# LN1's second transposes ahead of the last first-half products, weight sums behind its normalisation, residual offset added in the second f1/f2 chunk

## The chip, the cores and the metric

The kernel runs on one core of a Trainium2 chip. A core has a matrix engine (TensorE, PE), a vector engine (VectorE, DVE), a scalar engine (ScalarE, ACT), a general engine (GpSimd, POOL), and SyncE (SP), which here only issues loads. Each engine works through its own queue of instructions in order and waits on semaphores for the others. DMAs are issued from the queues of SP, ACT and POOL. The metric is the device time of one execution, in microseconds (us), as the median of several runs.

## What is computed

One layer of a decoder on 512 tokens of width 1024: a layer norm, a token mixer (gated linear attention beside latent attention), and a dense network, both with a scaled residual. The end of the reference, where the change lies:

```python
h = layer_norm(x, ln_in_g, ln_in_b)
mix = token_mixer(h, cos, sin, w_in[l], ...)
h = layer_norm(DEEPNORM_ALPHA * h + mix, ln1_g[l], ln1_b[l])
ff = jnp.square(jax.nn.relu(h @ w_ff1[l])) @ w_ff2[l]
h = layer_norm(DEEPNORM_ALPHA * h + ff, ln2_g[l], ln2_b[l])
```

`w_ff1` is 1024 x 4096 and `w_ff2` 4096 x 1024; `DEEPNORM_ALPHA` is 2 to the power 1/4.

## The kernel before

**Arithmetic.** Products are made of float32 operands split in two parts: `hi` is the operand rounded to the matrix engine's float32r, `lo` the rest. A product is hi·hi + hi·lo + lo·hi, so three matmuls (L245 to L247). Weights come by SP in tiles of 128 x 1024 (512 KB), and `pump` splits each one: ACT writes `whi` (L189), DVE subtracts to make `wlo` (L190).

**Order.** The program is written as a main thread that issues the matmuls, with generators beside it (`spawn`, `tick`, `finish`) that issue evictions, norms and transposes a step at a time. A scheduler then fixes the order of each engine's queue. `tc.issue_after(x)` makes what is written under it come behind the instruction x in that order. Once the queues are built, each is worked off in order.

**LN1.** After the mixer's output projection, `res` holds four tiles of 128 tokens by 1024. `ln1(0)` norms and transposes the tiles 0 and 1 (tokens 0 to 255, the first half), `ln1(1)` the tiles 2 and 3. In each, `ln_rows` takes mean and variance on DVE, raises the variance to the power −1/2 on POOL (L428) and normalises in place on DVE (L434). `ln_transpose` then makes, for each of eight k, two 128 x 128 transposes on PE (L443), the scaled `hi` on ACT (L446), an unrounded copy on ACT or DVE (L448, L450) and `lo` on DVE (L451). The results `h1T[k]` are the operand of f1.

**f1 of chunk 0.** While `ln1(1)` runs, PE does the f1 products of the first half: `gemm_fm` with `toks=slice(0, 256)`, eight k by four output blocks by three matmuls, 96 in all, each 256 wide. The same blocks are then run for the second half.

**f1 and f2 in chunks.** The hidden width of 4096 is taken in four chunks of 1024 (`FC = 4`). A chunk has f1 in blocks (`F1`), then f2. In the chunks 0 to 2, f2 is done by a scheme of seven products over quarters of the weight (`WIN`: 11, 21, T1, T2, T4, 22, T3). Its sums of quarters, T1 to T3, are made by `win_sums` on DVE (L1407), three for each half hf, and T4 during the products (L1460). The quarters are loaded by POOL's queue (`win_load`, L1399): chunk 0's before, those of chunk ci + 1 during f2 of chunk ci. From chunk 1 on the sums are held back behind the last evacuation of f2 (`st["ev"]`); those of chunk 0 aren't. The sums of hidden values are made by `win_hid` on DVE, and split by ACT and DVE (`xh`, `xl`).

**Evacuation.** Each of the seven products ends in two PSUM tiles. ACT copies each to an `ev` tile (L1471), and POOL issues one or more accumulating DMAs (L1473) that add it onto a 128 x 512 half of a `res` tile in SBUF. A chunk has 16 such DMAs of 256 KB.

**Residual.** `residual1` turns `res` from normalised rows to the scaled residual: it broadcasts `ln1_g` and `ln1_b` over the partitions by two DMAs on ACT's queue (`bcast_row`, L106), scales both by ALPHA on DVE (L1363, L1364), and multiplies each `res` tile by `bg` (L1365, L1369) and adds `bb` (L1370), all before f2 of chunk 0 starts. Addition onto `res` is commutative up to rounding, so the offset may be added at any time before the last norm.

Of the kernel before, what the change touches and what calls it, by code (L numbers as in the profile page):

```python
# [15 lines left out]
AF = mybir.ActivationFunctionType  # L16
ALU = mybir.AluOpType
AX = mybir.AxisListType

P = 128  # L20
T = 512
D = 1024
NT = T // P
# [12 lines left out]
ALPHA = 2.0 ** 0.25  # L36
# [16 lines left out]
def tile_hybrid_block(ctx: ExitStack, tc: tile.TileContext, I, out, dbg=None):  # L53
    nc = tc.nc
# [18 lines left out]
    def A(shape, dt=F32, n="a"):  # L73
        tag, bufs = ("C", 8) if n in TAG_C else (n, TAG_W[n]) if n in TAG_W else ("A", 24)
        return pa.tile(shape, dt, tag=tag, bufs=bufs, name=nm(n))

    def B(shape, dt=F32, n="b"):
        return pb.tile(shape, dt, tag="B", name=nm(n))

    def S(shape, dt=F32, n="s"):  # L80
        return sm.tile(shape, dt, tag=n, name=nm(n))
# [5 lines left out]
    def MM(n="mm"):  # L87
        return pm.tile([P, T], F32, tag="mm", name=nm(n))

    def PX(shape=(P, T), dt=F32, n="px"):  # L90
        return px.tile(list(shape), dt, tag="px", name=nm(n))

    def f(ap):
        return ap.bitcast(F32)

    act = nc.scalar.activation
    vtt = nc.vector.tensor_tensor
    vts = nc.vector.tensor_scalar
    stt = nc.vector.scalar_tensor_tensor
    gtt = nc.gpsimd.tensor_tensor  # L100
    mm = nc.tensor.matmul

    def bcast_row(name):
        t = A([P, D], F32, "bc")
        src = I[name]
        nc.scalar.dma_start(t, bass.AP(tensor=src.tensor, offset=src.offset, ap=[[0, P], [1, D]]))  # L106
        return t
# [21 lines left out]
    ident = ca[:, 0:P]  # L129
# [10 lines left out]
    st = {"dma": 0, "spl": 0, "gates": ()}  # L140
# [59 lines left out]
    def weights(pl, k):  # L200
        per = pl["per"]
        i = pl["idx"][k // per]
        pump(i)
        hi, lo = stream[i]["w"]
        return hi[:, k % per, :], lo[:, k % per, :]
# [4 lines left out]
    def spawn(g):  # L210
        active.append(g)
        return g
# [9 lines left out]
    def tick(width):  # L222
        for g in list(active[:width or WID[0]]):
            step(g)

    def finish(*gs):
        while any(g in active for g in gs):
            for g in list(active):
                if g in gs:
                    step(g)  # L230

    def part(x, i, c):
        return x[i][:, c] if isinstance(x, tuple) else x[:, i, c]

    def gemm_fm(pl, xs, n, evac, width=None, toks=slice(0, T), accs=None, guard=None):
        na = n // P
        accs = accs or [MM() for _ in range(na)]
        for k in range(pl["nk"]):
            hi, lo = weights(pl, k)
            xh, xl = part(xs[k], 0, toks), part(xs[k], 1, toks)  # L240
            first, last = k == 0, k == pl["nk"] - 1
            for a in range(na):
                c = slice(a * P, (a + 1) * P)
                o = accs[a][:, toks]
                mm(o, hi[:, c], xh, start=first, stop=False)  # L245
                mm(o, hi[:, c], xl, start=False, stop=False)  # L246
                mm(o, lo[:, c], xh, start=False, stop=last)  # L247
            if not last:
                tick(width)
        if guard:  # L250
            guard()
        if evac is not None:
            for a in range(na):
                evac(a, accs[a])
                if a == na // 2 - 1:
                    pump(pl["idx"][-1] + 1)
        tick(width)
        return accs
# [41 lines left out]
    PL = {}  # L300
# [121 lines left out]
    def ln_rows(src, dst, mv, on_act=False):  # L422
        bst = S([P, 2, 6], F32, "bst")
        for j in range(2):
            nc.vector.bn_stats(bst[:, j, :], src[:, j * T:(j + 1) * T])
        nc.vector.bn_aggr(mv, bst)
        vts(mv[:, 1:2], mv[:, 1:2], LN_EPS, None, op0=ALU.add)  # L427
        gtt(mv[:, 1:2], mv[:, 1:2], mhalf[:, 0:1], op=ALU.pow)  # L428
        if on_act:
            nmr = S([P, 1], F32, "nmr")  # L430
            stt(nmr, mv[:, 0:1], -1.0, mv[:, 1:2], op0=ALU.mult, op1=ALU.mult)
            act(dst, src, AF.Identity, scale=mv[:, 1:2], bias=nmr)
        else:
            vts(dst, src, mv[:, 0:1], mv[:, 1:2], op0=ALU.subtract, op1=ALU.mult)  # L434

    def ln_transpose(rows, g, b, outs, hf, alt=False, n="h0"):
        tk = slice(hf * 256, (hf + 1) * 256)
        for k in range(NK):
            if len(outs) <= k:
                outs.append(A([P, 2, T], F32R, n) if n == "h0" else (B([P, T], F32R, n), B([P, T], F32R, n)))  # L440
            p = MM() if alt and k in (4, 5) else PX()
            for i in range(2):
                nc.tensor.transpose(p[:, i * P:(i + 1) * P], rows[2 * hf + i][:, k * P:(k + 1) * P], ident)  # L443
            tmp = B([P, 256], F32, "lnt")
            hi, lo = part(outs[k], 0, tk), part(outs[k], 1, tk)
            ha = act(hi, p[:, :256], AF.Identity, scale=g[:, k:k + 1], bias=b[:, k:k + 1])  # L446
            if (alt or n == "h1") and k % 2:
                act(tmp, p[:, :256], AF.Identity, scale=g[:, k:k + 1], bias=b[:, k:k + 1])  # L448
            else:
                vts(tmp, p[:, :256], g[:, k:k + 1], b[:, k:k + 1], op0=ALU.mult, op1=ALU.add)  # L450
            hd = vtt(lo, tmp, f(hi), op=ALU.subtract)  # L451
            if n == "h1":
                st["ln"] = (ha, hd)
            yield hd
# [4 lines left out]
    def ln_in0():  # L459
        for tt in range(2):  # L460
            ln_rows(xt[tt], xt[tt], mvin[:, tt, :], on_act=tt == 0)
        yield from ln_transpose(xt, g_in, b_in, hT, 0, alt=True)
# [458 lines left out]
    scale = HQ ** -0.5  # L921
# [371 lines left out]
    t0, mv = mla_pair(0)  # L1293
# [3 lines left out]
    t1, mv = mla_pair(1)  # L1297
    mv(lambda: finish(*t0))
    t2, mv = mla_pair(2)
    mv(lambda: finish(*t1))  # L1300
    t3, mv = mla_pair(3)
    mv(lambda: finish(*t2))
    y_mla(0)
    res = []
# [33 lines left out]
    h1T = []  # L1338

    def ln1(hf):  # L1340
        for tt in (2 * hf, 2 * hf + 1):
            mv = S([P, 2], F32, "mv")
            ln_rows(res[tt], res[tt], mv)
        yield
        for k, _ in enumerate(ln_transpose(res, ln1g, ln1b, h1T, hf, n="h1")):
            if k % 2:
                yield
# [5 lines left out]
    finish(t_ln)  # L1353
    st["gates"] = st["ln"]
    t_ln = spawn(ln1(1))
    accs = gemm_fm(PL["f1", 0, 0], h1T, T, None, toks=slice(0, 256))
    finish(t_ln)

    def residual1():
        bg, bb = bcast_row("ln1_g"), bcast_row("ln1_b")  # L1360
        yield
        with tc.issue_after(st["ln"][1].ins):
            vts(bg, bg, ALPHA, None, op0=ALU.mult)  # L1363
            vts(bb, bb, ALPHA, None, op0=ALU.mult)  # L1364
            vtt(res[0], res[0], bg, op=ALU.mult)  # L1365
        yield
        for tt in range(NT):
            if tt:
                vtt(res[tt], res[tt], bg, op=ALU.mult)  # L1369
            vtt(res[tt], res[tt], bb, op=ALU.add)  # L1370
            yield

# [29 lines left out]
    def win_sums(ci):  # L1402
        def held(*a, **kw):
            with ExitStack() as gates:
                if "ev" in st:
                    gates.enter_context(tc.issue_after(st["ev"].ins))
                vtt(*a, **kw)  # L1407
        for hf in range(2):
            q12 = WQ.pop((("f2", ci), ("12", hf)))
            t1 = WQ[("f2", ci), ("T1", hf)] = A([P, 2, T], F32, "T1")  # L1410
            held(t1, q12, WQ[("f2", ci), ("11", hf)], op=ALU.subtract)
            yield
            held(q12, WQ[("f2", ci), ("22", hf)], q12, op=ALU.subtract)
            WQ[("f2", ci), ("T3", hf)] = q12
            yield
            t2 = WQ[("f2", ci), ("T2", hf)] = A([P, 2, T], F32, "T2")
            held(t2, q12, WQ[("f2", ci), ("11", hf)], op=ALU.add)
            yield
# [88 lines left out]
    for ci in range(FC):  # L1507
# [19 lines left out]
        for b, w in F1[ci]:  # L1527
            if ci == 0 and b == 0:
                gemm_fm(PL["f1", ci, b], h1T, T, ev_h, toks=slice(256, T), accs=accs)
                t_r1 = spawn(residual1())  # L1530
            else:
                gemm_fm(PL["f1", ci, b], h1T, w * P, ev_h, width=2)
            if win and b == 0:
                t_ws = spawn(win_sums(ci))
        if ci == 0:
# [6 lines left out]
        else:  # L1542
# [16 lines left out]
            rows = []  # L1559
# [7 lines left out]
            bg, bb = rows  # L1567
# [6 lines left out]
            tt, r, bst = 3, res[3], S([P, 4, 6], F32, "bst4")  # L1574
# [3 lines left out]
            for c0, n in ((0, T), (T, 256), (T + 256, 256)):  # L1578
                last = c0 > T
                acc = end if last else MM()[:, :n]  # L1580
                ws = slice(c0 % T, c0 % T + n)
                for k in range(nb):
                    hi, lo = weights(PL["f2last"][c0 // T], k)
                    xh, xl = hid[k][:, 0, tt * P:], hid[k][:, 1, tt * P:]
# [58 lines left out]
```

## Time and profile before

| what | value |
|---|---|
| median of three runs | 890.56 us (889.98 to 890.59) |
| time of the profiled execution | 890.77 us |
| its span in the profile | 888.9 us |
| granted TensorE clock | 0.999 |
| instructions | 12959 |

The profiled execution's time is 1.9 us longer than its span, which runs from the first to the last recorded instruction. All stamps below are microseconds from the span's start. A row of a timeline gives start, length, engine, line, operation, output <- inputs, shapes and count, and in brackets the idle time of the engine before it and what ended it. A row of the DMA view gives destination <- source, the issuing queue, the number of DMAs, the size of each and the median time from issue to landing. An engine's busy time is measured on its own; whether it costs anything is seen only where PE, the engine that is nearly always busy, waits.

### The profile page before, as it was taken

What the parts mean: (1) busy time and instruction counts of PE and PEld (TensorE: products, weight loads), DVE (VectorE), ACT (ScalarE), POOL (GpSimd) and SP (SyncE); (2) the same over time, 40 slices, a digit from 0 to 9 for tenths busy, and PEclk for the clock granted to TensorE, in tenths of its full rate; (3) what the DMA queues carried; (4) which work ended last, traced back from release to release, by engine and by line L of the source; (5) the groups of instructions that cost most, each with busy time, mean ns of one, the idle gap of its engine ahead of it and who ended that gap; (6) DMA issues with size and microseconds to landing.
All of it is one profiled execution on the core that took longest, in us unless ns stands there. A gap on an engine that the chain in (4) does not pass through costs nothing.

```text
span 888.9 us, 12959 instructions
## 1 busy us (share of the span) xinstructions
PE 870.0 (98%) x4844; PEld 757.6 (85%) x4844; DVE 629.8 (71%) x1011; ACT 468.8 (53%) x824; POOL 181.0 (20%) x198
## 2 busy tenths in 40 slices
PE   5999999999999999999999999999999999999996
PEld 5988887888899988888888888988888888889985
DVE  7859878967366745647766697887557646788865
ACT  5556666655366543535654424465457546656810
POOL 0324456725021010100000003004400520131001
PEclk9999999999999999999999999999999999999999
DMA  7995938234879433121307618005940990399312
GB/s 236 282 230 148 326 86 247 72 86 106 283 166 247 128 101 101 42 55 53 111 9 284 190 51 305 1 1 147 301 121 19 264 257 30 81 228 237 118 62 82
DMA packets 88414, 130.92 MB, mean 147 GB/s; under 512 B 8944, under 2 KB 50800, under 8 KB 88352
## 3 DMA queue, kind: packets, MB, share of 16 engines
q1 hardware_dynamic: 69120, 91.83, 32.7%
q0 software_dynamic: 17312, 34.61, 18.0%
q10 hardware_dynamic: 1920, 3.66, 1.1%
q8 instruction: 38, 0.62, 0.3%
q14 instruction: 24, 0.20, 0.1%
HBM read 108.58 MB, written 8.91 MB: 132 GB/s over the span
## 4 chain that ended last, share of the span: by engine, by line
PE 93%; POOL 2%; DVE 2%; issue 1%; DMA 1%; ACT 1%; POOLq 0%; SPq 0%; DVEq 0%; ACTq 0%
PE mm L245 12%; PE mm L247 12%; PE mm L246 12%; PE mm L279 6%; PE mm L281 6%; PE mm L280 6%; PE mm L1174 3%; PE mm L1173 3%; PE mm L1172 3%; PE px L1454 2%; PE px L1455 2%; PE px L1456 2%; PE mm L1455 2%; PE mm L1454 2%; PE mm L1456 2%; POOL rp L786 1%
## 5 line engine op out<-in xcount | busy, mean ns | idle before, releaser
L190 DVE TENSOR_TENSOR wlo<-wraw,whi 128x1024 fp32r<-128x1024 f32 (+2 forms) x93 | 103.9, 1118 | 98.8 <-ACT whi L189 93.8
L189 ACT ACTIVATE whi<-wraw 128x1024 fp32r<-128x1024 f32 (+2 forms) x93 | 88.7, 953 | 91.9 <-PE mm L246 40.4
L245 PE MATMUL mm<-h,whi 128*128 128x512 f32 x256 | 100.0, 391 | 0.0
L246 PE MATMUL mm<-h,whi 128*128 128x512 f32 x256 | 99.8, 390 | 0.0
L247 PE MATMUL mm<-h,wlo 128*128 128x512 f32 x256 | 95.2, 390 | 0.0
L190 DVE TENSOR_TENSOR wlo<-wq,whi 128x1024 fp32r<-128x1024 f32 x44 | 54.2, 1232 | 27.5 <-ACT whi L189 27.5
L1473 POOL DMA_DIRECT2D res<-ev x42 | 37.0, 1003 | 179.8 <-ACT ev L1471 146.2
L189 ACT ACTIVATE whi<-wq 128x1024 fp32r<-128x1024 f32 x44 | 46.4, 1056 | 23.7 <-PE mm L1173 9.9
L247 PEld LDWEIGHTS mm<-h,wlo 128*128 128x128 f32 x256 | 48.0, 188 | 10.3 <-DVE wlo L190 0.4
L245 PEld LDWEIGHTS mm<-h,whi 128*128 128x128 f32 x256 | 48.1, 188 | 9.8
L246 PEld LDWEIGHTS mm<-h,whi 128*128 128x128 f32 x256 | 48.1, 188 | 9.7
L1172 PE MATMUL mm<-sh,whi 128*128 128x256 f32 x160 | 45.4, 284 | 0.0
L1174 PE MATMUL mm<-sh,wlo 128*128 128x256 f32 x160 | 45.4, 284 | 0.0
L1173 PE MATMUL mm<-sh,whi 128*128 128x256 f32 x160 | 45.3, 283 | 0.0
L189 ACT ACTIVATE xh<-wraw 128x1024 fp32r<-128x1024 f32 (+1 forms) x28 | 27.2, 982 | 28.4 <-PE mm L281 15.7
L428 POOL TENSOR_TENSOR mv<-mv,mhalf 128x1 f32<-128x1 f32 x4 | 3.3, 838 | 170.5 <-DVE mv L427 170.5
L792 ACT ACTIVATE E<-rp 128x256 f32<-128x256 f32 x64 | 26.1, 419 | 22.3 <-POOL rp L787 13.8
L190 DVE TENSOR_TENSOR xl<-wraw,xh 128x1024 fp32r<-128x1024 f32 (+1 forms) x28 | 31.3, 1129 | 9.0 <-ACT xh L189 8.9
L1516 ACT ACTIVATE relu<-mm 128x512 f32<-128x512 f32 x24 | 14.1, 595 | 41.9 <-PE mm L247 41.9
L787 POOL TENSOR_TENSOR rp<-rp 128x256 f32<-128x256 f32 x32 | 32.3, 1010 | 11.6 <-ACT q L817 8.9
L786 POOL TENSOR_TENSOR rp<-rp 128x256 f32<-128x256 f32 x32 | 29.3, 916 | 20.2 <-ACT E L792 10.8
L794 DVE TENSOR_TENSOR M<-E,qk 128x512 f32<-128x512 f32 x32 | 28.9, 907 | 5.9 <-ACT E L792 5.9
(453 smaller groups left out, 2731.7 us busy)
## 6 DMA issues: line engine op xcount, KB each, us to landing
wraw<-in_w_ff_dram SPq DMA_DIRECT2D x36, 512.0 KB, 5.1
wraw<-in_w_in_dram SPq DMA_DIRECT2D x33, 512.0 KB, 4.0
wq<-in_w_ff_dram POOLq DMA_DIRECT2D x26, 512.0 KB, 9.7
res<-ev POOLq DMA_DIRECT2D x42, 256.0 KB, 10.0
wq<-in_w_in_dram SPq DMA_DIRECT2D x16, 512.0 KB, 6.2
wq<-in_w_in_dram POOLq DMA_DIRECT2D x16, 512.0 KB, 8.9
hsd<-hs SPq DMA_DIRECT2D x16, 256.0 KB, 4.1
xr<-hsd SPq DMA_DIRECT2D x16, 256.0 KB, 4.9
```

What stands on the lines that cost most here:

```text
L189: st["ins"] = act(hi[:, :nk, :n], raw[:, :nk, :n], AF.Copy)
L190: st["lo"] = vtt(lo[:, :nk, :n], raw[:, :nk, :n], f(hi[:, :nk, :n]), op=ALU.subtract)
L245: mm(o, hi[:, c], xh, start=first, stop=False)
L246: mm(o, hi[:, c], xl, start=False, stop=False)
L247: mm(o, lo[:, c], xh, start=False, stop=last)
L279: mm(o, xh, hi[:, :n], start=opens, stop=False, skip_group_check=share)
L280: mm(o, xh, lo[:, :n], start=False, stop=False, skip_group_check=share)
L281: mm(o, xl, hi[:, :n], start=False, stop=last, skip_group_check=share)
L786: gtt(Rv[:, :, 0, :], Rv[:, :, 0, :], Pv[:, :, 1, s - 1:s].to_broadcast([P, n, s]), op=ALU.add)
L1172: mm(oa, hi[:, k, c], xh, start=opens and k == 0 and a == 0, stop=False, skip_group_check=True)
L1173: mm(oa, hi[:, k, c], xl, start=False, stop=False, skip_group_check=True)
L1174: mm(oa, lo[:, k, c], xh, start=False, stop=k == 3, skip_group_check=True)
```

## The change

The change has three parts. (1) `gemm_fm` can hold its products from some k on behind an instruction; in the first-half f1 call the products of k = 6 and 7 (24 of 96) come behind the second half's transposes of k = 3. (2) The sums of chunk 0's weight quarters come behind LN1's last normalise. (3) `residual1` only multiplies by the gain; the offset's broadcast, its scaling (on ACT now, not DVE) and the four adds are made by a generator of their own, `offset1`, which is started in chunk 1 after the first f1 block's matmuls are issued.

```diff
+    def gemm_fm(pl, xs, n, evac, width=None, toks=slice(0, T), accs=None, guard=None, behind=None):
...
-            for a in range(na):
-                c = slice(a * P, (a + 1) * P)
-                o = accs[a][:, toks]
-                mm(o, hi[:, c], xh, start=first, stop=False)
...
+            with ExitStack() as gates:
+                if behind and k >= behind[0]:
+                    gates.enter_context(tc.issue_after(st[behind[1]].ins))
+                for a in range(na):
+                    c = slice(a * P, (a + 1) * P)
+                    o = accs[a][:, toks]
+                    mm(o, hi[:, c], xh, start=first, stop=False)
...
-            vts(dst, src, mv[:, 0:1], mv[:, 1:2], op0=ALU.subtract, op1=ALU.mult)
+            return vts(dst, src, mv[:, 0:1], mv[:, 1:2], op0=ALU.subtract, op1=ALU.mult)
...
-                nc.tensor.transpose(p[:, i * P:(i + 1) * P], rows[2 * hf + i][:, k * P:(k + 1) * P], ident)
+                t = nc.tensor.transpose(p[:, i * P:(i + 1) * P], rows[2 * hf + i][:, k * P:(k + 1) * P], ident)
+            if k == 3:
+                st["tr"] = t
...
-            ln_rows(res[tt], res[tt], mv)
+            st["aff"] = ln_rows(res[tt], res[tt], mv)
...
-    accs = gemm_fm(PL["f1", 0, 0], h1T, T, None, toks=slice(0, 256))
+    accs = gemm_fm(PL["f1", 0, 0], h1T, T, None, toks=slice(0, 256), behind=(6, "tr"))
...
     def residual1():
-        bg, bb = bcast_row("ln1_g"), bcast_row("ln1_b")
+        bg = bcast_row("ln1_g")
         yield
         with tc.issue_after(st["ln"][1].ins):
             vts(bg, bg, ALPHA, None, op0=ALU.mult)
-            vts(bb, bb, ALPHA, None, op0=ALU.mult)
             vtt(res[0], res[0], bg, op=ALU.mult)
         yield
+        for tt in range(1, NT):
+            vtt(res[tt], res[tt], bg, op=ALU.mult)
+            yield
+
+    def offset1():
+        bb = bcast_row("ln1_b")
+        yield
+        act(bb, bb, AF.Copy, scale=ALPHA)
+        yield
         for tt in range(NT):
-            if tt:
-                vtt(res[tt], res[tt], bg, op=ALU.mult)
             vtt(res[tt], res[tt], bb, op=ALU.add)
             yield
...
-                if "ev" in st:
-                    gates.enter_context(tc.issue_after(st["ev"].ins))
+                gates.enter_context(tc.issue_after(st["ev" if "ev" in st else "aff"].ins))
                 vtt(*a, **kw)
...
+            if ci == 1 and b == 0:
+                spawn(offset1())
             if win and b == 0:
                 t_ws = spawn(win_sums(ci))
```

More of the change, by code (lines that the diff above doesn't have):

```diff
@@ L233, in part @@
         return x[i][:, c] if isinstance(x, tuple) else x[:, i, c]
-    def gemm_fm(pl, xs, n, evac, width=None, toks=slice(0, T), accs=None, guard=None):
+    def gemm_fm(pl, xs, n, evac, width=None, toks=slice(0, T), accs=None, guard=None, behind=None):
         na = n // P
@@ L241, in gemm_fm @@
             first, last = k == 0, k == pl["nk"] - 1
-            for a in range(na):
-                c = slice(a * P, (a + 1) * P)
-                o = accs[a][:, toks]
-                mm(o, hi[:, c], xh, start=first, stop=False)
-                mm(o, hi[:, c], xl, start=False, stop=False)
-                mm(o, lo[:, c], xh, start=False, stop=last)
+            with ExitStack() as gates:
[5 more added lines that the diff above has]
+                    mm(o, hi[:, c], xh, start=first, stop=False)
+                    mm(o, hi[:, c], xl, start=False, stop=False)
+                    mm(o, lo[:, c], xh, start=False, stop=last)
             if not last:
```

## The prediction

> **What bounds the kernel now.** I read the page first: totals, the chain that ended last, the DMA issues.
>
> ```profile
> span 888.9 us, 12959 instructions
> PE 870.0 (98%) x4844; PEld 757.6 (85%) x4844; DVE 629.8 (71%) x1011; ACT 468.8 (53%) x824; POOL 181.0 (20%) x198
> PE 93%; POOL 2%; DVE 2%; issue 1%; DMA 1%; ACT 1%; POOLq 0%; SPq 0%; DVEq 0%; ACTq 0%
> res<-ev POOLq DMA_DIRECT2D x42, 256.0 KB, 10.0
> ```
>
> TensorE (PE) is busy for 98% of the span and carries 93% of the chain. The change removes no product, so it can gain only where PE stands still and lose only where it makes PE stand still. Next the table by stretches of time (columns: stretch, length, then PE, PE weight load, DVE, ACT, POOL busy us with counts, granted clock, DMA share, GB/s), for LN1 with the first f1 products, for the end of chunk 0's f1, and for chunk 1's f1.
>
> ```profile
> 548.50:566.00 17.50, 17.15 (x140) 16.58 (x139) 14.52 (x27) 6.30 (x12) 1.85 (x2) 1.00 0.29 103
> 575.00:596.00 21.00, 21.00 (x95) 17.37 (x93) 19.95 (x30) 13.57 (x23) 0.00 (x0) 1.00 0.00 1
> 640.00:680.00 40.00, 40.00 (x178) 33.16 (x177) 21.65 (x30) 23.16 (x35) 3.60 (x5) 1.00 0.40 98
> ```
>
> PE idles only in the first stretch: 17.50 − 17.15 = 0.35 us, more than that when counted start to start, because the end of a matmul is modelled. In the third, PE takes one 512-wide product every 40.00/178 = 0.225 us and never stops. The timeline of PE in LN1 shows the stall (start, length, instruction, and in brackets the idle time before it and its releaser).
>
> ```profile
> 560.13 0.29 PE L247 MATMUL mm<-h,xl 128*128 128x256 f32 x1
> 560.26 1.03 PE L443 MATMUL px<-ca,res 128*128 128x128 f32 x8
> 561.62 0.74 PE L245 MATMUL mm<-h,xh 128*128 128x256 f32 x4 [0.33 <-ACT h L446]
> 562.20 0.44 PE L443 MATMUL px<-ca,res 128*128 128x128 f32 x2
> 562.66 0.39 PE L246 MATMUL mm<-h,xh 128*128 128x256 f32 x1
> 562.88 0.28 PE L247 MATMUL mm<-h,xl 128*128 128x256 f32 x1
> 563.72 0.64 PE L245 MATMUL mm<-h,xh 128*128 128x256 f32 x4
> ```
>
> The 96 first-half products end at 560.13 with a product's pitch of 560.26 − 560.13 = 0.13 (0.12 where they run in rows). Eight transposes of the second half follow, and the products of that half wait for ACT's eviction of them. Eight transposes at some 0.108 last until 561.13, so 0.49 is lost before 561.62; the smaller steps up to 563.72 (four products at 0.12 from 561.62 to 562.10 with the transposes only at 562.20, and three like it) add some 0.45. The stall is about 0.95 us.
>
> **The change, part by part.** *(1) Gate on the last 24 first-half products, weight sums behind the normalisation.* The second half's transposes of k = 0 to 3 go ahead of the 24 products of k = 6 and 7, so these 24 × 0.12 = 2.9 us cover the evictions that were waited for. That needs the normalised rows by 560.26 − 2.9 = 557.4. DVE and POOL in that place:
>
> ```profile
> 553.99 1.85 POOL L428 TENSOR_TENSOR mv<-mv,mhalf 128x1 f32<-128x1 f32 x2 [9.93 <-DVE mv L427]
> 554.20 1.22 DVE L1407 TENSOR_TENSOR T<-wq,wq 128x1024 f32<-128x1024 f32 x1
> 555.46 1.23 DVE L1407 TENSOR_TENSOR wq<-wq,wq 128x1024 f32<-128x1024 f32 x1
> 556.60 1.53 DVE L434 TENSOR_SCALAR res<-res,mv 128x1024 f32<-128x1024 f32 x2
> ```
>
> POOL's two pow end at 555.84. The two normalises are over at 558.13, because a weight sum (to 556.69) runs ahead of them. Behind the gate on them the sums come after, and 555.84 + 1.53 = 557.4, with the first row tile done half of that earlier: just in time. Transposes issue at the same count, earlier; no DMA moves. I take the whole 0.95 (bounds 0 and 0.95). The sums are pushed back 1.5 us on a DVE that has their products due only in f2, after 596.
>
> *(2) Offset out of residual1.* DVE loses there one bias scale and four adds:
>
> ```profile
> 568.13 0.69 DVE L1364 TENSOR_SCALAR bc<-bc 128x1024 f32<-128x1024 f32 x1
> 573.27 3.49 DVE L1370 TENSOR_TENSOR res<-res,bc 128x1024 f32<-128x1024 f32 x3
> 577.81 1.22 DVE L1370 TENSOR_TENSOR res<-res,bc 128x1024 f32<-128x1024 f32 x1
> ```
>
> That is 0.69 + 3.49 + 1.22 = 5.4 us of DVE between 568 and 579, while PE does not stop (21.00 busy of 21.00 behind it): worth nothing by itself.
>
> *(3) The adds in chunk 1.* Between 568 and 579 nothing wrote `res`. In chunk 1 the accumulating DMAs of f2's chunk 0 write it, and each add of a res tile waits until the last of these has landed. POOL's issues of that chunk, the tile view's row of the last six (shortest, median and longest issue in ns, first and last start), and the times to landing of the first and of the last of these:
>
> ```profile
> 607.98 1.84 POOL L1473 DMA_DIRECT2D res<-ev  x2 [52.15 <-ACT ev L1471]
> 615.22 5.30 POOL L1399 DMA_DIRECT2D wq<-in_w_ff_dram  x7
> 637.49 0.85 POOL L1473 DMA_DIRECT2D res<-ev  x1 [5.65 <-DMA res<-ev]
> 639.26 4.35 POOL L1473 DMA_DIRECT2D res<-ev  x5 [0.92 <-DMA res<-ev]
> L1473 POOL DMA_DIRECT2D res<-ev x6: 847/1151/1862, 637.5 to 642.5; - x6
> res<-ev POOLq DMA_DIRECT2D x1, 256.0 KB, 6.5
> res<-ev POOLq DMA_DIRECT2D x1, 256.0 KB, 10.3
> ```
>
> The last six land from 637.49 + 6.5 = 644.0 to 642.5 + 10.3 = 652.8, so 8.8/5 = 1.76 apart: a stream at its own pace. In DVE's new order these adds stand in line with chunk 1's f1 weights: the fourth add (res[3]), then one weight sum, then the subtraction that makes `wlo` of an f1 weight tile; I call it tile E. DVE is in order, so all of it waits for the last landing. Its slack:
>
> ```profile
> 640.81 1.23 DVE L190 TENSOR_TENSOR wlo<-wraw,whi 128x1024 fp32r<-128x1024 f32 x1 [3.44 <-ACT whi L189]
> 646.28 1.23 DVE L190 TENSOR_TENSOR wlo<-wraw,whi 128x1024 fp32r<-128x1024 f32 x1 [4.24 <-ACT whi L189]
> 650.62 0.39 PE L245 MATMUL mm<-h,whi 128*128 128x512 f32 x1
> 651.53 0.62 PE L247 MATMUL mm<-h,wlo 128*128 128x512 f32 x2
> ```
>
> Tile E's first product is the row at 650.62. Its `wlo` was ready at 647.51 and PE first needs it at 651.53: 4.0 us of slack. With a landing at L it is ready at L + 1.22 (add) + 1.22 (sum) + 1.23 less two overlaps of 0.08 = L + 3.5. If L stayed at 652.8, that is 656.3 and PE stands until then: +4.8 against today, whatever LN1 gained, because the end of this wait is set by DMA, not by PE. The tile before it (subtracted at 640.81, due 24 products of 0.225 before tile E's, at 646.1) has the first add ahead of it: 644.0 + 1.22 + 1.23 = 646.4 at worst, 0.3 late and swallowed by the next wait.
>
> *(4) What moves L.* The new order of PE brings the first evacuation of f2 chunk 0 behind 36 products, not 48: 12 × 0.225 = 2.7 us earlier, plus 0.95 from LN1. ACT and POOL there:
>
> ```profile
> 604.31 2.00 ACT L189 ACTIVATE xh<-T 128x1024 fp32r<-128x1024 f32 x2
> 607.08 1.09 ACT L1471 ACTIVATE ev<-px 128x512 f32<-128x512 f32 x2 [0.78 <-PE px L1456]
> 612.47 0.60 ACT L1471 ACTIVATE ev<-px 128x512 f32<-128x512 f32 x1 [1.17 <-DMA res<-ev]
> ```
>
> The second pair of evacuations waits for the first pair's landing, and the seven weight loads and the rest of POOL's queue come after it. So a first pair 3.4 us earlier (3.65 less a split that is now ahead of it on ACT for part of it) brings L to 652.8 − 3.4 = 649.4, unless ACT is held in between. And ACT now has, before that second pair, the scale of `bb`, which waits for its own 512 KB broadcast, issued by ACT at about 602.4 (one `xh` split of 1 us ahead of the row at 604.31, less 0.95). Bounds of its price: the four bc loads of before, and an SP load of equal size on quiet queues.
>
> ```profile
> bc<-in_ln_in_g_dram ACTq DMA_DIRECT2D x1, 512.0 KB, 8.0
> bc<-in_ln_b_dram ACTq DMA_DIRECT2D x2, 512.0 KB, 10.0
> wraw<-in_w_ff_dram SPq DMA_DIRECT2D x1, 512.0 KB, 3.8
> L1314 ACT ACTIVATE bc<-bc x1: 1060/1060/1060, 480.1 to 480.1; 128x1024 f32<-128x1024 f32 x1
> ```
>
> The first two ran beside other loads. At 602 the queues are quiet (0.00 DMA share up to 596) but for one SP load that comes at about the same time, so I take a value near the quiet end, 3.8 to 5.2. At 3.8 it lands at 606.2, when ACT is done with the evacuations (605.6): ACT loses 1.06 + 0.6, which its idle time before 607.08 and 612.47 (0.78 + 1.17) covers. L = 649.4, `wlo` ready at 652.9, net 652.9 − 651.5 = +1.4. At 5.2, 607.6: the second pair comes some 1.2 later, L = 650.6, net +2.6. I forecast between: +1.8, that is 890.77 + 1.8 = 892.6 for the profiled run, which lies 0.2 above the median, and so 892.4.
>
> [...]
>
> **Rivals.** *A: ACT is held by the broadcast.* It takes the loaded price, 8.0 to 10.0: it lands at 610.4 to 612.4, `bb` is scaled by 611.5 to 613.5, two more splits (1.05 each) follow, and the second pair evacuates at 613.6 to 615.6 instead of 612.47, so L is 1.1 to 3.1 later than before: net +5.9 to +7.9; between this and the forecast (a landing at 608 to 610) lies +3 to +5. For it: all bc rows. Against it: quiet queues. About 894 to 898.5.
>
> *B, the other side: the slack takes the adds.* From L below 651.53 − 0.95 − 3.5 = 647.1 on PE does not wait and only the gain of LN1 is left: 890.56 − 0.95 = 889.6. The stream would have to run 5.7 us earlier, by the two pairs' waits falling away altogether; for it stands that landings, not work, delay the second pair (1.17 idle); against it the 1.76 spacing behind POOL's seven loads.
>
> *C: the gate does not do what it says.* The normalises are ready later than 557.4 (the pow rows, 1.85 for two, are rough), PE waits on the transposes instead of the evictions. LN1 gains nothing; L is 0.95 later; net +2.4 to +3.5: 893.0 to 894.1.
>
> **How the numbers follow.** Forecast 0.55 (891.8 to 893.2), A with what lies between 0.27, B 0.12, C 0.06. The range runs from B's 889.6 to 896.5, into A: about 0.12 is left out above and 0.04 below. A difference under 0.2% (1.8 us, below 888.8 or above 892.3) is what a measurement here can't tell from none. Faster by more would need twice LN1's stall: 0.04. B and the lower half of the forecast are "same": 0.40. The upper half, A and C: 0.56.
>
> **What would show it.** In the new profile: no idle time of PE over 0.2 us between 555 and 566 (part 1); the normalises ahead of the sums; the add of res[3] on DVE released by a DMA res<-ev at 649 to 651, and a PE idle time of 2 to 4 us before the wlo product near 651 to 654, released by DVE wlo; ACT's scale of `bc` idle before it under 2 us (A: over 4). The prediction is wrong if PE has no idle time there (B), if L is later than 651.5 (A), or if a stall appears in another place, such as the T sums due in f2.

## The result, and the profile after

| | before | after |
|---|---|---|
| median, us | 890.61 (889.98 to 891.03, 6 runs) | 894.93 (894.37 to 895.39, 6 runs) |
| profiled execution, us | 890.77 | 895.39 |
| its span, us | 888.9 | 893.4 |

The changed kernel is slower: ratio 1.0048, 95% interval 1.0038 to 1.0058, or 4.3 us. The forecast was 892.4 within 889.6 to 896.5.

The page of the changed kernel, the totals, the chain that ended last, and the group of products with `wlo` (busy us, mean ns | idle time before them, releaser):

```profile
span 893.4 us, 12964 instructions
PE 872.0 (98%) x4844; PEld 758.6 (85%) x4844; DVE 629.1 (70%) x1010; ACT 470.5 (53%) x825; POOL 181.6 (20%) x198
PE 82%; issue 7%; DMA 5%; POOL 3%; DVE 2%; ACT 1%; POOLq 0%; SPq 0%; DVEq 0%; ACTq 0%
L250 PE MATMUL mm<-h,wlo 128*128 128x512 f32 x256 | 96.1, 394 | 3.7 <-DVE wlo L190 3.7
```

PE still does 4844 instructions, but its share of the chain fell from 93% to 82%, and DMA, 1% before, now has 5%: the chain now runs back through transfers for part of the way. The products with `wlo` idle 3.7 us for DVE, where they idled for nothing before.

**LN1.** The timeline of PE and then of DVE in the changed kernel:

```profile
556.98 1.04 PE L446 MATMUL px<-ca,res 128*128 128x128 f32 x8
560.72 0.38 PE L446 MATMUL px<-ca,res 128*128 128x128 f32 x2
560.85 0.60 PE L248 MATMUL mm<-h,xh 128*128 128x256 f32 x3
561.29 0.82 PE L446 MATMUL px<-ca,res 128*128 128x128 f32 x6
561.86 0.36 PE L249 MATMUL mm<-h,xh 128*128 128x256 f32 x1
```

```profile
554.17 1.70 DVE L437 TENSOR_SCALAR res<-res,mv 128x1024 f32<-128x1024 f32 x2 [0.31 <-POOL mv L431]
555.79 1.22 DVE L1417 TENSOR_TENSOR T<-wq,wq 128x1024 f32<-128x1024 f32 x1
```

No row of PE has idle time before it. The normalises end at 555.87, ahead of the sums, and the transposes start at 556.98. From the first f1 product to the first f2 product it took 596.22 − 548.74 = 47.48 us before and 594.88 − 548.35 = 46.53 now: LN1 gave 0.95 us. (The other 0.4 by which the stamps are earlier is there before LN1, a difference of the two executions: in all but one of the profiles the first f1 product lies somewhere between 548.1 and 549.1.)

**Chunk 1.** DVE, then PE, in the changed kernel. The bracket on an add names the landing that it waited for. I call the f1 weight tile before tile E tile D.

```profile
643.24 1.23 DVE L1381 TENSOR_TENSOR res<-res,bc 128x1024 f32<-128x1024 f32 x1 [7.29 <-DMA res<-ev]
644.38 1.22 DVE L190 TENSOR_TENSOR wlo<-wraw,whi 128x1024 fp32r<-128x1024 f32 x1
646.54 1.23 DVE L1381 TENSOR_TENSOR res<-res,bc 128x1024 f32<-128x1024 f32 x1 [0.94 <-DMA res<-ev]
649.16 1.23 DVE L1381 TENSOR_TENSOR res<-res,bc 128x1024 f32<-128x1024 f32 x1 [1.39 <-DMA res<-ev]
650.66 1.22 DVE L1381 TENSOR_TENSOR res<-res,bc 128x1024 f32<-128x1024 f32 x1 [0.28 <-DMA res<-ev]
651.92 1.22 DVE L1417 TENSOR_TENSOR T<-wq,wq 128x1024 f32<-128x1024 f32 x1
653.06 1.22 DVE L190 TENSOR_TENSOR wlo<-wraw,whi 128x1024 fp32r<-128x1024 f32 x1
```

```profile
644.52 0.39 PE L249 MATMUL mm<-h,whi 128*128 128x512 f32 x1
645.65 0.73 PE L250 MATMUL mm<-h,wlo 128*128 128x512 f32 x2 [0.74 <-DVE wlo L190]
...
651.00 0.39 PE L249 MATMUL mm<-h,whi 128*128 128x512 f32 x1
654.33 0.73 PE L250 MATMUL mm<-h,wlo 128*128 128x512 f32 x2 [2.95 <-DVE wlo L190]
...
655.83 0.59 PE L249 MATMUL mm<-h,whi 128*128 128x512 f32 x1
656.22 0.63 PE L250 MATMUL mm<-h,wlo 128*128 128x512 f32 x1
656.64 0.63 PE L248 MATMUL mm<-h,whi 128*128 128x512 f32 x1
```

DVE idles 7.29 us for the landing of res[0], with tile D's `wlo` queued behind it, and PE waits from 644.75 to 645.65. Then res[3]'s landing, the add, the sum and E's `wlo` (ready at 654.28), and PE waits from 651.23 to 654.33. The first `wlo` product of tile E was at 651.53 before: it is 2.8 us late, or 3.2 when the 0.4 between the two executions is taken out. The rest comes behind it: from 656.22 on products are 0.43 us apart, not 0.225. The windows view of the changed kernel shows why (the same columns as before; the clock is the third number from the end):

```profile
651.00:654.33 3.33, 0.39 (x2) 0.00 (x0) 3.30 (x4) 0.35 (x1) 0.00 (x0) 1.00 0.01 5
654.33:655.83 1.50, 1.50 (x6) 1.24 (x7) 1.50 (x5) 0.00 (x0) 0.00 (x0) 1.00 0.25 46
655.83:659.20 3.37, 3.37 (x9) 2.61 (x8) 3.07 (x5) 1.06 (x1) 0.00 (x0) 0.51 0.50 150
659.20:662.00 2.80, 2.80 (x14) 2.30 (x13) 0.29 (x1) 1.87 (x3) 0.00 (x0) 0.99 0.50 170
```

For 3.4 us PE is busy throughout but was granted half the clock. Eight products spaced 0.2 us too wide make 1.6. In all 2.8 + 1.6 = 4.4, against 4.5 between the two spans and 4.3 between the medians.

### The profile page after: what moved, and what is told of

It reads as the page before. It is cut to its first block, busy times and chain, and to the rows that moved or that the text cites. A ratio compares the mean times of both kernels' runs of the same rounds, so it can differ in the third digit from the quotient of the medians.

```text
span 893.4 us, 12964 instructions
## 1 busy us (share of the span) xinstructions
PE 872.0 (98%) x4844; PEld 758.6 (85%) x4844; DVE 629.1 (70%) x1010; ACT 470.5 (53%) x825; POOL 181.6 (20%) x198
## 4 chain that ended last, share of the span: by engine, by line
PE 82%; issue 7%; DMA 5%; POOL 3%; DVE 2%; ACT 1%; POOLq 0%; SPq 0%; DVEq 0%; ACTq 0%
PE mm L250 10%; PE mm L248 10%; PE mm L249 10%; PE mm L282 6%; PE mm L283 6%; PE mm L284 6%; PE mm L1179 3%; PE mm L1178 3%; PE mm L1177 3%; DMA res<-ev 3%; PE px L1465 2%; PE px L1466 2%; PE px L1464 2%; DMA wq<-in_w_ff_dram 1%; PE mm L1465 1%
```

## The experiments

The kernel before was run again beside each group, and the ratios are to those runs: its median was 890.59 beside the experiments 1 to 4, 890.84 beside 5 to 8, and 890.66 beside 9 and 10.

**1. Parts 1 and 2 alone.** `residual1` as before, no `offset1`.

```diff
+        bg, bb = bcast_row("ln1_g"), bcast_row("ln1_b")
-            if ci == 1 and b == 0:
-                spawn(offset1())
```

> Parts 1 and 2 alone: residual1 adds the offset before f2 of chunk 0 as before. If the loss comes from the adds in chunk 1, only LN1's gain is left: PE reached the tile products of chunk 1 0.88 us earlier in the changed kernel (644.30 against 645.18), so 889.5 to 889.9 us, no idle time of PE between 555 and 566 nor between 640 and 660, granted clock 1.00 throughout 640 to 662. Rival: the gain at LN1 is only a shift that later waits take back, or the gates of parts 1 and 2 delay the sums due in f2: then 890.4 to 891.

Measured: 889.70 us (11 runs), ratio 0.9990 (0.9981 to 0.9999). Its windows view has PE without a gap in both places, at a clock of 1.00:

```profile
555.00:566.00 11.00, 11.00 (x95) 11.00 (x95) 9.55 (x17) 5.80 (x12) 0.76 (x1) 1.00 0.01 3
640.00:662.00 22.00, 22.00 (x98) 18.22 (x98) 12.07 (x19) 14.27 (x21) 4.15 (x5) 1.00 0.75 178
```

The gain at LN1 is real and kept to the end, 890.59 − 889.70 = 0.89 us, and the whole loss belongs to part 3. (The 0.88 of the expectation sets two different products of tile D against each other: the one at 644.30 stands against 645.64, not 645.18. That is 1.34, of which 0.95 is LN1's and 0.4 lies between the executions.)

**2. Part 3 alone**, `residual1` and `offset1` as in the change, on the kernel before.

```diff
+            if ci == 1 and b == 0:
+                spawn(offset1())
```

> Part 3 alone: LN1 as before, the offset added in chunk 1. If the whole loss is of part 3 and the accumulating stream moves with PE, the last landing comes 0.9 us later than in the changed kernel (650.57), at about 651.5, PE waits for the wlo of tile E until some 655.2, and the slow stretch of 1.5 us follows: 895.4 to 896.1. Rival: the landing does not move with PE (the stream has a pace of its own), and the time is that of the changed kernel, 894.7 to 895.1. If parts 1 and 2 carry some of the loss: under 894.3.

Measured: 898.22 us (897.27 to 900.77, 5 runs), ratio 1.0092 (1.0080 to 1.0105). Slower than either theory said. Its PE timeline in LN1 has the cause:

```profile
561.00 0.73 PE L245 MATMUL mm<-h,xh 128*128 128x256 f32 x4 [0.33 <-ACT h L446]
562.37 1.35 PE L443 MATMUL px<-ca,res 128*128 128x128 f32 x8 [0.63 <-ACT lnt L448]
564.29 0.39 PE L246 MATMUL mm<-h,xh 128*128 128x256 f32 x1 [0.57 <-DVE h L451]
```

Without part 2's gate the scheduler now puts more weight sums in among LN1's evictions, and PE waits three times. From the first f1 product to the first f2 product it takes 49.09 us, 1.6 more than before. So PE reaches f2 at 597.21, 2.3 later than in the changed kernel, and the last landing comes at 653.4, not 650.6: the issue that ends the six starts at 644.39 and takes 9.0. E's `wlo` is ready at 655.86 + 1.22 = 657.1, 5.6 later than its need in the kernel before, and a slow stretch follows (a granted clock of 0.53 from 657.13 to 660.53), 5.6 + 1.6 = 7.2, against 7.3 between the spans and 7.6 between the medians. The landings do move with PE, as the forecast had it. What I missed is that taking work off DVE changes where the scheduler puts the other work.

**3. The adds spread.** The same adds behind the `wlo` of later tiles.

```diff
+        at = {0: 4, 1: 5, 2: 6, 3: 7}
+        w = [i for b, _ in F1[1] for i in PL["f1", 1, b]["idx"]]
         for tt in range(NT):
-            vtt(res[tt], res[tt], bb, op=ALU.add)
+            with ExitStack() as gates:
+                if tt in at:
+                    while "loi" not in stream[w[at[tt]]]:
+                        yield
+                    gates.enter_context(tc.issue_after(stream[w[at[tt]]]["loi"].ins))
+                vtt(res[tt], res[tt], bb, op=ALU.add)
```

(`pump` keeps each tile's `wlo` subtraction as `e["loi"]`.)

> The change with the four adds put behind the wlo subtractions of the f1 tiles 4 to 7 of chunk 1, one behind each (E is tile 3), everything else as it is. All landings are over by 650.6, before the first of these adds. If it was the place in DVE's queue, not the adds' work, that cost time, PE has no idle time over 0.2 us and no slow stretch between 640 and 690, and the time is 889.5 to 889.9. Rival: four adds of 1.22 us in chunk 1 are too much for DVE whatever their place, and later wlo or xl come late: 890.5 to 893.

Measured: 889.85 us (11 runs), ratio 0.9993 (0.9984 to 1.0002). Its windows view:

```profile
640.00:662.00 22.00, 22.00 (x99) 18.22 (x98) 13.40 (x20) 12.77 (x19) 1.96 (x3) 1.00 0.66 157
662.00:690.00 28.00, 28.00 (x125) 23.21 (x124) 24.11 (x30) 18.66 (x27) 1.74 (x2) 1.00 0.15 35
```

PE has no gap, though DVE does the same four adds in the same chunk. What cost 4.3 us in the change was their place in DVE's queue, in front of work that was due, and not their 4.9 us of work. It does no better than parts 1 and 2 alone (889.70): moving the offset is worth nothing here.

**4. First add behind tile D.** As 3, with `at = {0: 2}`.

> The change with the first add put behind the wlo subtraction of tile D (tile 2), so D's wlo no longer waits for a landing; the scheduler then puts the weight sum behind tile E's wlo. D's stall of 1.0 us goes; tile E's wlo still waits for the last landing (650.6) but without the sum of 1.22 in between: ready at about 653.0, so PE stands from 650.6 to 653.0, 2.4 us in one piece against 1.0 and 3.1. Stalls alone: 1.3 us less than the changed kernel, 893.6. If the slow stretch (granted clock 0.51 for 3.4 us) follows any stall over 1 us, it stays and the time is 893.4 to 893.8; if it needs a stall of about 3 us, it goes and the time is 891.9 to 892.4.

Measured: 896.87 us (895.03 to 898.82, 5 runs), ratio 1.0073 (1.0059 to 1.0087): the expectation missed, the wait grew instead of shrinking. In the profiled execution, the fastest of the five, E's `wlo` starts at 652.84 and PE waits 3.5 us in one piece, as the last landing came 1.0 later than in the changed kernel (the issue at 641.40 took 10.2). The expectation had taken that landing as fixed, and it isn't. In the three profiles in which tile D's `wlo` waits for res[0] (the changed kernel and the experiments 2 and 9), the last six landings are 1.41 to 1.47 us apart; they are 1.76 apart in the kernel before, 1.7 in experiment 7 and 1.74 here. SP's next weight load starts as soon as D's `wlo` is done, at 641.16 here and at 645.62 in the changed kernel, so it may be this load that slows the landings; that was not tested. The windows around the wait:

```profile
650.40:654.10 3.70, 0.39 (x2) 0.00 (x0) 3.19 (x4) 0.35 (x1) 0.00 (x0) 1.00 0.03 7
654.28:657.70 3.42, 3.42 (x10) 2.63 (x10) 3.39 (x8) 0.07 (x1) 0.00 (x0) 0.56 0.49 153
```

The slow stretch is there, 3.4 us long again (the second window begins before it, so the clock shows as 0.56). The runs of this version differ by 3.8 us; what made the other four still longer was not profiled and stays open.

**5 and 6. Each of the parts 1 and 2 by itself**, on the kernel of experiment 1: first without part 2's gate, then without `behind=(6, "tr")`.

```diff
-                gates.enter_context(tc.issue_after(st["ev" if "ev" in st else "aff"].ins))
+                if "ev" in st:
+                    gates.enter_context(tc.issue_after(st["ev"].ins))
```

> Part 1 alone: the last 24 first-half products behind the transposes, but the weight sums of chunk 0 not held behind the normalise, and residual1 as before. If each of the parts 1 and 2 needs the other, the normalises end near 558.1 as before, PE reaches the transposes at 557.2 and now waits for the normalise instead of the evictions: 890.3 to 890.8, no gain that can be told from none. Rival: the gate on PE alone removes the stall of 0.95: 889.5 to 889.9, as parts 1 and 2 together (889.70).

```diff
-    accs = gemm_fm(PL["f1", 0, 0], h1T, T, None, toks=slice(0, 256), behind=(6, "tr"))
+    accs = gemm_fm(PL["f1", 0, 0], h1T, T, None, toks=slice(0, 256))
```

> Part 2 alone: the weight sums behind the normalise, the first-half products in their old place. The rows are normalised earlier, but PE comes to the transposes only at 560.2 and still waits for their evictions: the stall of 0.5 to 0.95 stays, 890.3 to 890.8. Rival: what PE waited for was DVE busy with sums at the evictions, and holding these back frees it: 889.5 to 889.9.

Measured: part 1 alone 890.15 (11 runs), ratio 0.9994 (0.9985 to 1.0002); part 2 alone 891.40 (11 runs), ratio 1.0010 (1.0001 to 1.0019). PE of part 2 alone:

```profile
561.19 0.74 PE L248 MATMUL mm<-h,xh 128*128 128x256 f32 x4 [0.33 <-ACT h L451]
561.77 0.44 PE L446 MATMUL px<-ca,res 128*128 128x128 f32 x2
563.01 0.44 PE L446 MATMUL px<-ca,res 128*128 128x128 f32 x2 [0.81 <-ACT lnt L453]
```

From the first f1 product to the first f2 product it takes 46.98 us with part 1 alone, 48.33 with part 2 alone, 46.55 with both and 47.48 before. So part 1 alone has about half of the gain, 0.50 us; the rest goes to a wait for the normalise. Its times agree (0.7 less than the kernel before beside it), but its interval doesn't exclude no gain. Part 2 alone loses: the eviction wait stays, and the weight sums that were held back now fall among the evictions and add 1.0 at 563.01. Part 2 helps only where part 1 is.

**7. Two adds ahead.** As 3, with `at = {0: 2, 3: 3}`.

> The change with the first add behind tile D's wlo and the fourth behind tile E's, so D waits for no landing, and E's wlo waits for the landing of res[2], not of res[3] (about 649.1 to 649.9 against 650.6 to 651.6 in the profiles so far). E's wlo is ready at 651.4 to 652.3; PE needs it at 650.7: one stall of 0.8 to 1.6 us. If landings set the time, the stall shrinks by what the landing is earlier. If a stall must be longer than that for the slow stretch (granted clock 0.51), the time is 889.7 + 0.8 to 1.6 = 890.5 to 891.3; if any stall of a us brings it, 892 to 892.9.

Measured: 893.05 us (892.06 to 897.03, 8 runs), ratio 1.0034 (1.0021 to 1.0046). In the profile, PE waits 1.9 us for E's `wlo`, and then:

```profile
653.01:656.40 3.39, 3.39 (x10) 2.61 (x9) 3.39 (x8) 0.00 (x0) 0.00 (x0) 0.51 0.51 155
656.40:660.00 3.60, 3.60 (x17) 2.99 (x16) 2.47 (x3) 2.12 (x3) 0.00 (x0) 0.99 0.32 86
```

The wait shrank with the landing, and the slow stretch stayed at full size: here a wait of 1.9 us was enough for it. Three of the eight runs lie between 894.3 and 897.0; they were not profiled.

**8. A stall made by DVE.** The version of 3, with E's subtraction computed four times.

```diff
+                for _ in range(3 if st["spl"] == PL["f1", 1, 2]["idx"][1] else 0):
+                    vtt(lo[:, :nk, :n], raw[:, :nk, :n], f(hi[:, :nk, :n]), op=ALU.subtract)
```

> The version with the spread adds (889.85), and tile E's wlo subtraction computed four times over on DVE, the same values each time, so that PE waits for it with no DMA concerned: DVE then has the next tile's wlo and an add ahead of the last of the four, and it ends near 655, a stall of about 4.2 us in one piece. If the slow stretch follows a stall of PE whatever causes it, a stretch of 3.4 us at a granted clock of about 0.5 comes after it, worth 1.5, and the time is 889.85 + 4.2 + 1.5 = 895.5; if the slow stretch has to do with the accumulating DMAs landing at that time, the clock stays at 1.00 and the time is 894.0.

Measured: 890.88 us (889.72 to 896.17, 12 runs), ratio 1.0009 (0.9997 to 1.0020). It decides nothing: the scheduler let PE run later products first, and PE waited only 0.7 us in all in the profile. Two of the twelve runs lie at 894.2 and 896.2; they were not profiled, and why is open. Their mean granted clocks, 0.996 and 0.995, are the lowest of the twelve, which fits a slow stretch but doesn't show one.

**9. Last add behind tile E.** As 3, with `at = {3: 3}`.

> The change with only the fourth add behind tile E's wlo. Tile D's wlo waits for the landing of res[0] as in the changed kernel (ready 645.3 to 645.65, due 644.75), tile E's for the landing of res[2] as in the version with two adds ahead (ready about 652.2, due 651.4 after D's stall). PE reaches the same point as there, but its wait comes in two pieces of 0.6 to 0.9 us in place of one of 1.94. If only a long wait in one piece brings the slow stretch, the granted clock stays at 1.00 and the time is 889.7 + 1.5 = 891.0 to 891.5, some 1.5 to 2 under the version with two adds ahead (893.05); if what counts is PE's idle time summed over some us, or the landings, it stays and the time is 892.7 to 893.3.

Measured: 891.48 us (889.57 to 894.02, 11 runs), ratio 1.0008 (0.9999 to 1.0017), 1.6 less than with two adds ahead (1.4 when each is set against the kernel before beside it), though E's `wlo` hangs on the same landing of res[2]. Its windows view:

```profile
644.00:662.00 18.00, 17.14 (x75) 13.59 (x75) 12.30 (x15) 6.83 (x11) 1.23 (x2) 1.00 0.70 156
```

PE waits 1.0 us for tile D here, and the clock stays at 1.00 over the whole stretch. But the profiled execution, 894.02, is the longest of the eleven: it also waited some 2.1 us in LN1's first half, from 545 on, where weights came late. PE was so late by then that E's `wlo` (ready at 654.52) came in time for it (654.58), and the second piece of the wait is not in this trace. That two short waits bring no slow stretch is supported by the times of the other runs, and not shown by a profile.

**10. The stall held.** The version of 8, with PE's later products kept behind E's first ones.

```diff
+                if pl is PL["f1", 1, 2] and k >= 5 or pl is PL["f1", 1, 4]:
+                    gates.enter_context(tc.issue_after(st["last"].ins))
...
-                    mm(o, lo[:, c], xh, start=False, stop=last)
+                    t = mm(o, lo[:, c], xh, start=False, stop=last)
+            if pl is PL["f1", 1, 2] and k in (4, 7):
+                st["last"] = t
```

> The version with the spread adds, tile E's wlo subtraction computed four times over on DVE as in the run before, and PE's products of the next k and the next block held behind those of tile E's first k, so that PE can't run ahead as it did there. The last subtraction ended at 654.67 there; PE needs it at 650.7: a wait of 3.6 to 4.0 us in one piece, caused by DVE's work and no landing. If the slow stretch follows PE's wait whatever causes it: 3.4 us at a granted clock near 0.5 after it, 889.85 + 3.8 + 1.5 = 895.2 (894.7 to 895.8). If it has to do with the accumulating DMAs: clock 1.00, 893.4 to 893.9.

Measured: 895.53 us (894.85 to 897.39, 5 runs), ratio 1.0055 (1.0043 to 1.0068). PE's row and the windows of this kernel:

```profile
654.50 0.73 PE L254 MATMUL mm<-h,wlo 128*128 128x512 f32 x2 [3.62 <-DVE wlo L192]
```

```profile
650.49:654.50 4.01, 0.40 (x3) 0.01 (x1) 4.01 (x6) 0.36 (x1) 0.00 (x0) 1.00 0.25 72
655.20:658.60 3.40, 3.40 (x10) 2.63 (x9) 1.22 (x1) 0.67 (x1) 0.00 (x0) 0.50 0.55 161
658.60:662.00 3.40, 3.40 (x16) 2.79 (x16) 0.13 (x1) 1.71 (x3) 0.00 (x0) 1.00 0.00 0
```

The last landing, at 651.42, falls into this wait, but neither PE nor DVE waits for it, and the same 3.4 us at half clock come. In experiment 3 the last landing comes at 651.84 without a wait of PE, and the clock stays at 1.00. So the slow stretch follows PE's standing still, be it for a landing or for DVE's work, and not the landings.

## Why the prediction was right, and the term it lacked

**The time: inside the range, in part by luck.** 894.93 is above the forecast's own band of 891.8 to 893.2. The range held it because it reached up to 896.5 for rival A, and A did not happen. What filled that room instead were a wait 1.0 longer than forecast and 1.5 to 1.6 us at half clock that the prediction did not have.

**LN1: right.** A gain of 0.95 was forecast, 0.95 came (0.89 between the medians of experiment 1). The normalises were ready at 555.9, not 557.4.

**The wait that takes its place: right in mechanism and place, too small.** The fourth add did hold E's `wlo` until the last landing, L. This was forecast at 649.4 to 650.6 and came at 650.57. E's `wlo` was ready at L + 3.7, not L + 3.5, and E's first `wlo` product came 2.8 later than before, where +1.8 was forecast within +1.4 to +2.6.

**What moved L: right in part, and its value in part luck.** ACT and the broadcast in the changed kernel, timeline and DMA view:

```profile
601.04 0.33 ACTq L106 DMA_DIRECT2D bc<-in_ln_b_dram  x1
603.02 1.09 ACT L1481 ACTIVATE ev<-px 128x512 f32<-128x512 f32 x2
604.94 1.06 ACT L1378 ACTIVATE bc<-bc 128x1024 f32<-128x1024 f32 x1
609.37 0.60 ACT L1481 ACTIVATE ev<-px 128x512 f32<-128x512 f32 x1 [0.56 <-DMA res<-ev]
```

```profile
bc<-in_ln_b_dram ACTq DMA_DIRECT2D x1, 512.0 KB, 3.7
```

The broadcast took 3.7, the quiet price, and ACT never waited for it: neither rival A nor the upper price of 5.2 came about. No run shows the 5.2 behind the forecast's +2.6: ACT began to scale the broadcast 3.9 after its issue, without a wait, in the changed kernel and in the experiments 2 and 4. A broadcast beside other loads was hardly put to the test, as SP's load began only 2.2 us after it. By the price of 3.7 L should have been 649.4, at the lower end; it came at the upper end, which had been worked out for a broadcast that holds up the second pair. The first pair of evacuations came 4.1 earlier and the second 3.1, but the first of the last six landings only 0.8 (643.21 against 644.0): the weight loads and accumulations in between, which the chain of waits shows back to back, took longer. The six then landed 1.47 apart, not 1.76, so that the last came 2.2 earlier. My lower price for L took the whole shift of the first pair through to the end and the spacing of 1.76 as the stream's own; both steps were wrong, and their errors partly cancel.

**Tile D: too small.** It was put at 0.3 late at worst. It was 0.9: the add of res[0] starts at 643.24, its landing 0.8 earlier than the 644.0 of before, but PE needs D's `wlo` at 644.75, 1.3 earlier than 646.09. That E's wait swallows it held, since E's `wlo` hangs on the last landing. A stall in another place was one of the prediction's own signs of being wrong, and this is one.

**The term that was not there.** The step "net 652.9 − 651.5" took PE to go on at full speed from the moment E's `wlo` is ready. The runs showed 1.5 to 1.6 us more: the granted clock halves for 3.4 us soon after the wait. With it the forecast's upper case of +2.6 would have been +4.2, and 4.3 was measured; the +1.8 would have been +3.4. **Rival B** (the slack takes the adds) would have needed a landing before 647.1. **Rival C** is excluded by experiment 1.

## What to carry to other kernels

An operation moved to "where there is room" is placed in a queue, and what counts is what it waits for and who stands behind it: an add of 1.2 us with an accumulating DMA ahead of it blocked an in-order engine for 7 us in a chunk where that engine was half idle. Look up the time to landing of the last writer before you choose the place, and put the operation behind the work that is due. And a stall of the matrix engine can cost more than its length: here five waits of 1.9 to 3.8 us cost 1.5 to 1.6 us more, while one of 1.9 and shorter ones did not.

## What the runs showed of the hardware

The slow stretch was not expected. Five profiles have one, after waits of PE of 1.9, 3.1, 3.1, 3.5 and 3.8 us; each is 3.4 us long at a granted clock of 0.50 to 0.56, and costs 1.5 to 1.6. It begins between 0.2 and 1.5 us after PE goes on, and not at the wait's start. There is none after the single waits of 0.9 us (tile D in the changed kernel) and 1.0 us (tile D in experiment 9), nor after the 2.1 us in experiment 9's profile, 1.9 of them in one piece: the windows behind them have a clock of 1.00. So length alone does not decide near 2 us.

The traces point to what does. In those of the two kernels the changes of the granted clock lie whole multiples of 3.4133 us apart. In the changed kernel the clock is recorded as full from 14.16 on, the slow stretch begins at 655.86 (188 such periods later) and ends at 659.28 (one more), and the clock is halved again at 891.38 (68 more), after PE's last product; in the kernel before it is full from 12.70 and halved at 886.52 (256 later), again after the last product. The windows view by such periods, first around the wait of 1.9 us in experiment 7, then around that of 1.9 us in experiment 9:

```profile
649.63:653.05 3.42, 1.65 (x8) 1.05 (x7) 3.26 (x3) 0.77 (x1) 0.00 (x0) 1.00 0.25 58
653.05:656.46 3.41, 3.41 (x10) 2.63 (x9) 3.41 (x8) 0.00 (x0) 0.00 (x0) 0.50 0.51 154
```

```profile
542.77:546.19 3.42, 2.51 (x12) 1.70 (x11) 0.14 (x1) 1.23 (x2) 1.78 (x3) 1.00 1.01 393
546.19:549.60 3.41, 2.52 (x14) 1.81 (x14) 3.38 (x7) 3.41 (x9) 0.00 (x0) 1.00 1.04 379
```

The first wait lies within the period before the slow one. With a period's end taken at 546.19, the second, nearly as long, is cut into 1.1 and 0.8 us, and no slow period follows; as the clock is 1.00 on both sides, this view doesn't show that place itself. In all five cases PE stood still for 1.9 us or more (1.9, 1.9, 2.7, 2.9 and 3.1) in the 3.4 us right before the slow stretch; in the changed kernel that is 652.44 to 654.33, only 1.9 of the 3.1 us. In the traces of the two kernels, past the first 20 us, no period with 1.5 us or less of standing still has a slow one behind it. This is a reading of these traces; no experiment moved a wait within a period, so what a wait's place in a period does was not shown by itself.
